# An HGRN layer by pairs of heads: the in-projection in seven products for eight

## The chip, the cores and the metric

The kernel runs on one core of one Trainium2 chip. The metric is device time in microseconds from start to end of one execution; the profile's busy times, waits and chains come from one execution taken by the hardware profiler. The engines are PE (matrix products), DVE (vector operations), ACT (functions and copies), POOL (a further vector engine) and SP, which here only issues the loads and stores.

## The reference, cut to what matters

A two-layer trunk is run over 1024 prompt frames and 32 frames of a running stream: an SSD layer, a SwiGLU FFN, an HGRN layer, a second FFN, a final norm. The change is in the HGRN layer, whose computation is:

```
proj = h @ in_w                       # (L, 1024) @ (1024, 4096)
q, f, i, g = split(proj, 4)           # 8 heads of 128 each
q = silu(q);  forget = lb + (1 - lb) * sigmoid(f);  k = 1 - forget;  logg = log(forget)
per head and chunk:  b = cumsum(logg)
    sc = mask(q*exp(b) @ (k*exp(-b))^T);  o = sc @ v + q*exp(b) @ S
    S = exp(b_last) * S + (k*exp(b_last - b))^T @ v
o = o * rsqrt(mean(o*o) + eps) * gnorm_w * silu(g)
out = o @ out_w                       # added to the residual x
```

Inputs and outputs are float32. The outputs include the carried states.

## The kernel before

**Layout.** Activations lie transposed, features on the 128 partitions and frames along the free axis. The 1056 frames are two halves: half one has 512, half two has 512 of the prompt and the 32 of the stream, 544 together (`LEN`). A block is what one matmul streams: 512 columns in half one, 272 twice in half two (`BLK`).

**Products.** Each float32 operand is split into a rounded part and a remainder (`split`, `wsplit`: a copy on ACT, a subtraction on DVE), and each product is made as three matmuls: high by high, high by low, low by high (`product`, lines 314 to 316). Weights come by DMA into `raw` (three buffers), the split weights lie in `ws` (six buffers).

**HGRN layer.** `hgrn_layer` walks 16 units, half by half, head by head. For a head, `hgrn_proj` makes one of the four parts (f, q, v, g) as a plain product of 1024 features by 128 outputs. `hgrn_f` turns f into the decay (tanh, Ln, a scan over frames at line 753, two Exp) and the keys. `hgrn_chunk` and `hgrn_chunk_b` run over four chunks of 128 frames (a fifth of 32 in half two): scores, mask, two transposes, the state's update, the output. `hgrn_gate` norms the head's output through a sum over partitions (a product with ones, line 331), Ln and Exp, and multiplies by the gate. `hgrn_out` makes the output projection of two heads and adds it to the residual (`accumulate`).

**Order.** The code is written as a list of tasks per unit that are dealt out between the chunks: g of this head, the output projection of the last two heads, f, q and v of the next head. A scheduling layer then sets the order on each engine, with some functions lifted in priority (`lifted`). Each engine runs its own list in order; semaphores tie them.

**FFN.** The FFN's gate and up products already run as units (`ffn_unit`, `unit_weights`): a matrix of 1024 by 256 weights is cut into four blocks, and seven products of sums of blocks stand for the eight (`part`, lines 993 to 995). `x_combos` makes the sums of x that these need, `unit_weights` the four sums of weights, on DVE. `in_turn` alternates the steps of two units.

Of the kernel before, what the change touches and what calls it, by code (L numbers as in the profile page):

```python
# [42 lines left out]
FIXED = 14368  # L43
BUFS = {"x": 12, "ys": 8, "cb": 4, "xd": 2, "de": 2, "ec": 2, "ss": 1, "xr": 2, "n": 4, "w": 3}
# [4 lines left out]
def trunk_kernel(ctx, tc, x_prompt, x_sample, state_ssd, cache_conv, state_hgrn,  # L49
# [85 lines left out]

    smalls, hec = [place(P) for _ in range(6)], [place(16) for _ in range(3)]
# [80 lines left out]
    cw = place(96)  # L217
    cc = place(72)
    dtb = place(1)
    acol = place(1)  # L220
    dcol = place(16)
# [30 lines left out]
    def other_vectors():  # L252
        rows = T("n", "rows")[:, :P]
        for c, src in ((C_FFN, ffn_norm_w), (C_HGN, hgrn_norm_w), (C_GN, ssd_gnorm_w),
                       (C_HG, hgrn_gnorm_w), (C_LB, hgrn_lower_bounds)):
            n = src.shape[0] * src.shape[1] // P
            dma(rows[c - NV0:c - NV0 + n, :], src.rearrange("o (m p) -> (o m) p", p=P))
        columns(rows, NVC - NV0, vc[:, NV0:])
        V.tensor_scalar_mul(vc[:, C_GN:C_HG + 1], vc[:, C_GN:C_HG + 1], 0.5)
# [76 lines left out]
    colt = place(5 * P)  # L336
# [64 lines left out]
    carry = place(NCT * 3).rearrange("p (a b) -> p a b", b=3)  # L401
    newc = place(2 * 3 * NCT).rearrange("p (a b c) -> p a b c", b=3, c=NCT)
# [21 lines left out]
    def ssd_dt(h, xn, blocks):  # L424
# [34 lines left out]
        lastc = place(5)  # L459
# [6 lines left out]
        elast = place(160).rearrange("p (h c) -> p h c", c=5)  # L466
# [181 lines left out]
    def ssd_layer(after, w0):  # L648
# [12 lines left out]
        for i, (h, g) in enumerate(units):  # L661
# [12 lines left out]
            else:  # L674
                tasks = zs + after[:1] + outs + after[1:]
# [39 lines left out]

    def half_two_norm():
# [7 lines left out]
    Sh = [Shb[e // 4][:, (e % 4) * P:(e % 4 + 1) * P] for e in range(8)]  # L724

    HB2 = 1
# [3 lines left out]
    def hgrn_proj(h, e, part, evac):  # L730
        col = (part * 8 + e) * P
        w = wload([(0, P, hgrn_in_w[0][:, col:col + P])], KD, P)
        for (b0, bn) in BLK[h]:
            ps = psum_mm()
            product(ps, w, 0, xns[h], b0, bn)
            evac(slice(b0, b0 + bn), ps[:, :bn])

    def silu2(t):
        def f(s, ps):
            act(t[:, s], ps, AF.Tanh, scale=0.5)  # L740
            stt(t[:, s], t[:, s], 1.0, ps, ADD, MUL)
        return f

    @lifted("hf")
    def hgrn_f(h, e, u):

        L = LEN[h]
        th = T("w", "hth")
        hgrn_proj(h, e, 1, lambda s, ps: act(th[:, s], ps, AF.Tanh, scale=0.5))
        d, b, k = T("w", "hlg"), T("w", "hb"), T("ys", "hk")  # L750
        act(d[:, :L], th[:, :L], AF.Ln, scale=c1[:, e:e + 1], bias=c0[:, e:e + 1])
        ts(k[:, :L], th[:, :L], nc1[:, e:e + 1], c1[:, e:e + 1], MUL, ADD)
        V.tensor_tensor_scan(out=b[:, :L], data0=rmask[:, :L], data1=d[:, :L], initial=0.0,
                             op0=MUL, op1=ADD)
        b3 = b[:, :H1].rearrange("p (c t) -> p c t", t=P)
        tt(d[:, :H1].rearrange("p (c t) -> p c t", t=P), b3,
           b3[:, :, MID:MID + 1].to_broadcast([P, 4, P]), SUB)
        if h:
            tt(d[:, H1:L], b[:, H1:L], b[:, MIDS:MIDS + 1].to_broadcast([P, NS]), SUB)
        ec = small("hec", 16)  # L760
        V.tensor_copy(ec[:, 0:4], b[:, MID:H1:P])
        V.tensor_copy(ec[:, 5:9], d[:, P - 1:H1:P])
        if h:
            V.tensor_copy(ec[:, 4:5], b[:, MIDS:MIDS + 1])
            V.tensor_copy(ec[:, 9:10], d[:, L - 1:L])
        else:
            V.memset(ec[:, 4:5], 0.0)
            V.memset(ec[:, 9:10], 0.0)
        tt(ec[:, 10:13], ec[:, 5:8], ec[:, 1:4], ADD)
        act(ec[:, :13], ec[:, :13], AF.Exp)  # L770
        ep, em = T("n", "hep"), T("n", "hem")
        act(ep[:, :L], d[:, :L], AF.Exp)
        act(em[:, :L], d[:, :L], AF.Exp, scale=-1.0)
        tt(k[:, :L], k[:, :L], em[:, :L], MUL)
        u.update(k=k, ep=ep, ec=ec)

    def hgrn_q(h, e, u):
        L = LEN[h]
        q = T("ys", "hq")
        hgrn_proj(h, e, 0, silu2(q))  # L780
        stt(q[:, :L], q[:, :L], 0.5, u["ep"][:, :L], MUL, MUL)
        u["q"] = q

    def hgrn_v(h, e, u):
        v = T("ys", "hv")
        hgrn_proj(h, e, 2, lambda s, ps: act(v[:, s], ps, AF.Copy))
        u["v"] = v

    def hgrn_g(h, e, u):
        g = T("xd", "hg")  # L790
        hgrn_proj(h, e, 3, silu2(g))
        u["g"] = g

    @lifted("hchunk")
    def hgrn_chunk(h, e, c, u):
# [17 lines left out]
        kv = T("xr", "hkv")  # L813
# [29 lines left out]
    @lifted("hgate")  # L843
    def hgrn_gate(h, e, u):
        L = LEN[h]
        ot = u["o"]
        r = rstd_of([ot[:, :L]], BLK[h], 1.0 / P, L)
        stt(ot[:, :L], ot[:, :L], vc[:, C_HG:C_HG + 1], r[:, :L], MUL, MUL)
        tt(ot[:, :L], ot[:, :L], u["g"][:, :L], MUL)
        yp = u["yp"]  # L850
        u["y"] = split(ot[:, :L], L, (yp[:, 2 * (e % 2)], yp[:, 2 * (e % 2) + 1]))

    def hgrn_out(h, e2, m4, ys):
        w = wload([(0, 512, hgrn_out_w[0][e2 * 256:(e2 + 1) * 256, m4 * 512:(m4 + 1) * 512])], 2, 512)
        for mi in range(4):
            for (b0, bn) in BLK[h]:
                ps = psum_mm()
                product(ps, w, mi * P, ys, b0, bn)
                accumulate(h, m4 * 4 + mi, ps, b0, bn)

    def hgrn_layer(after):
        units = [(h, e) for h in range(2) for e in range(8)]
        us = [{"S": None} for _ in units]
        r = []
        for f in (hgrn_f, hgrn_q, hgrn_v):
            f(0, 0, us[0])
        for i, (h, e) in enumerate(units):
            u = us[i]
            tasks = [lambda: hgrn_g(h, e, u)]
            if e % 2 == 0 and i:  # L870
                ph, pe = units[i - 1]
                tasks += [lambda m4=m4: hgrn_out(ph, pe // 2, m4, [us[i - 2]["y"], us[i - 1]["y"]])
                          for m4 in range(2)]
            if i + 1 < len(units):
                nh, ne = units[i + 1]
                tasks += [lambda f=f: f(nh, ne, us[i + 1]) for f in (hgrn_f, hgrn_q, hgrn_v)]
            if (h, e) == (0, 5):
                tasks.append(lambda: r.append(x_stat(1, st[2])))
            if (h, e) == (0, 6):
                tasks = mixed(tasks, norm_pieces(1, C_HGN, xns[1], ((0, LEN[1]),), r[0], XN2))  # L880
            if (h, e) == (1, 6):
                tasks += after[:1]
            if (h, e) == (1, 7):
                tasks += after[1:]
            u["o"] = T("ys", "ho")
# [419 lines left out]
```

## Time and profile before

| | |
|---|---|
| median of 3 runs | 2886.57 us (2885.68 to 2887.0) |
| the profiled execution | 2887.34 us, its span 2885.6 us |
| PE busy | 2843.3 us, 99% of the span |
| DVE busy | 2152.4 us, 75% |
| ACT busy | 1556.9 us, 54% |
| POOL busy | 43.5 us, 2% |
| granted clock of PE | 0.997 |

The HGRN layer lies about between 1556 and 2181 us. In a row of a group the columns are: line, engine, operation, output and inputs by the program's names, shapes, count, then busy microseconds and mean nanoseconds of one, then the engine's idle time before them and what ended it. In a row of the timeline the columns are start and duration in microseconds, then the instruction.

### The profile page before, as it was taken

The page shows a single profiled execution, that of the slowest core. Times are in us where ns is not written, and L with a number is a line of the kernel's source. Part 1 is how long each engine was busy: PE and PEld are TensorE (multiplying, and loading weights), DVE is VectorE, ACT ScalarE, POOL GpSimd, SP SyncE. Part 2 cuts the span into 40 slices and gives each one's busy share as a digit, 9 for nine tenths or more (in the row PEclk, how much of TensorE's full clock was granted, in tenths as well). Part 3 has the DMA queues.
Part 4 walks back from the last instruction along what each step waited for, and adds up shares of the span by engine and source line. Part 5 has one row for each costly group of instructions (what it writes and reads, how often), then busy time and mean ns, then how long its engine had stood idle before and what let it go on. Part 6 is the DMA issues. An engine that isn't in the chain of part 4 may idle for free.

```text
span 2885.6 us, 49044 instructions
## 1 busy us (share of the span) xinstructions
PE 2843.3 (99%) x19711; PEld 2618.5 (91%) x19711; DVE 2152.4 (75%) x3744; ACT 1556.9 (54%) x2922; POOL 43.5 (2%) x156
## 2 busy tenths in 40 slices
PE   7999999999999999999999999999999999999998
PEld 7777788999988999999999887899989999999998
DVE  6787797787787877897777556655568877887777
ACT  5665554554653744455444656555564644454445
POOL 0000000000100000000000000000000000000000
PEclk9999999999999999999999999999999999999999
DMA  5543334444332333323333222222223333333223
GB/s 152 137 111 106 98 88 123 113 112 101 107 86 88 110 104 95 110 84 102 95 96 107 81 74 66 76 78 78 73 78 95 110 96 103 107 96 96 88 89 112
DMA packets 401246, 282.60 MB, mean 98 GB/s; under 512 B 22633, under 2 KB 388730, under 8 KB 401018
## 3 DMA queue, kind: packets, MB, share of 16 engines
q1 hardware_dynamic: 401018, 279.47, 33.5%
q8 instruction: 154, 2.52, 0.4%
q14 instruction: 74, 0.61, 0.1%
HBM read 271.61 MB, written 7.82 MB: 97 GB/s over the span
## 4 chain that ended last, share of the span: by engine, by line
PE 92%; DVE 5%; ACT 1%; issue 1%; DMA 1%; SPq 0%; POOL 0%; DVEq 0%; ACTq 0%
PE mm L314 19%; PE mm L315 19%; PE mm L316 19%; PE mm L995 5%; PE mm L993 5%; PE mm L994 5%; PE sc L995 4%; PE sc L993 4%; PE sc L994 4%; PE sc L594 1%; PE sc L583 1%; PE sc L331 1%; PE sc L580 1%; DVE fixed L101 1%; PE sc L822 1%
## 5 line engine op out<-in xcount | busy, mean ns | idle before, releaser
L98 ACT ACTIVATE wh<-raw 128x512 fp32r<-128x512 f32 (+1 forms) x688 | 557.4, 818 | 604.8 <-PE mm L315 474.2
L314 PE MATMUL mm<-xn,wh 128*128 128x272 f32 (+2 forms) x1552 | 524.9, 338 | 0.0
L315 PE MATMUL mm<-xn,wh 128*128 128x272 f32 (+2 forms) x1552 | 519.3, 335 | 5.2 <-issue 5.2
L316 PE MATMUL mm<-xn,wl 128*128 128x272 f32 (+2 forms) x1552 | 518.3, 334 | 0.9 <-DVE wl L101 0.9
L101 DVE TENSOR_TENSOR wl<-raw,wh 128x1024 fp32r<-128x1024 f32 x308 | 375.8, 1222 | 82.9 <-ACT wh L98 59.3
L101 DVE TENSOR_TENSOR fixed<-mm,fixed 128x272 f32<-128x272 f32 (+1 forms) x512 | 263.2, 525 | 192.0 <-PE mm L316 190.2
L314 PE MATMUL mm<-fh,wh 128*128 128x272 f32 (+1 forms) x1056 | 341.6, 325 | 1.2 <-DVE fixed L101 0.9
L315 PE MATMUL mm<-fl,wh 128*128 128x272 f32 (+1 forms) x1056 | 341.9, 324 | 0.8 <-DVE fl L101 0.8
L316 PE MATMUL mm<-fh,wl 128*128 128x272 f32 (+1 forms) x1056 | 341.6, 324 | 0.0
L316 PEld LDWEIGHTS mm<-xn,wl 128*128 128x128 f32 x1552 | 293.4, 189 | 34.6 <-issue 6.9
L314 PEld LDWEIGHTS mm<-xn,wh 128*128 128x128 f32 x1552 | 293.3, 189 | 29.3 <-issue 2.8
L315 PEld LDWEIGHTS mm<-xn,wh 128*128 128x128 f32 x1552 | 293.2, 189 | 27.6 <-issue 1.2
L101 DVE TENSOR_TENSOR wh<-raw,wh 128x512 fp32r<-128x512 f32 x380 | 256.7, 688 | 41.5 <-ACT wh L98 38.8
L993 PE MATMUL mm<-th,wh 128*128 128x272 f32 (+1 forms) x912 | 260.4, 286 | 0.0
L995 PE MATMUL mm<-th,wh 128*128 128x272 f32 (+1 forms) x912 | 259.7, 285 | 0.0
L994 PE MATMUL mm<-tl,wh 128*128 128x272 f32 (+1 forms) x912 | 259.6, 285 | 0.0
L314 PEld LDWEIGHTS mm<-fh,wh 128*128 128x128 f32 x1056 | 198.3, 188 | 17.6 <-DVE fixed L101 1.8
L315 PEld LDWEIGHTS mm<-fl,wh 128*128 128x128 f32 x1056 | 198.7, 188 | 16.4 <-DVE fl L101 1.8
L316 PEld LDWEIGHTS mm<-fh,wl 128*128 128x128 f32 x1056 | 198.7, 188 | 15.2
L993 PE MATMUL sc<-xn,wh 128*128 128x272 f32 (+1 forms) x608 | 173.2, 285 | 0.5 <-ACT wh L98 0.5
L993 PEld LDWEIGHTS mm<-th,wh 128*128 128x128 f32 x912 | 171.8, 188 | 1.7 <-ACT s L98 0.9
L994 PE MATMUL sc<-xn,wh 128*128 128x272 f32 (+1 forms) x608 | 173.2, 285 | 0.0
(251 smaller groups left out, 6627.5 us busy)
## 6 DMA issues: line engine op xcount, KB each, us to landing
raw<-in_ffn_w_down_dram SPq DMA_DIRECT2D x90, 512.0 KB, 3.4
raw<-in_ffn_w_gate_dram SPq DMA_DIRECT2D x88, 512.0 KB, 4.1
raw<-in_ffn_w_up_dram SPq DMA_DIRECT2D x88, 512.0 KB, 4.6
raw<-in_ssd_in_w_dram SPq DMA_DIRECT2D x80, 512.0 KB, 4.1
raw<-in_hgrn_in_w_dram SPq DMA_DIRECT2D x64, 512.0 KB, 4.2
cumB<-cumd SPq DMA_DIRECT2D x64, 256.0 KB, 4.4
raw<-in_ssd_out_w_dram SPq DMA_DIRECT2D x32, 512.0 KB, 4.0
raw<-in_hgrn_out_w_dram SPq DMA_DIRECT2D x16, 512.0 KB, 3.4
```

What stands on the lines that cost most here:

```text
L98: A.activation(out=out, in_=in_, func=f, **kw)
L101: (eng or V).tensor_tensor(out=out, in0=a, in1=b, op=op)
L314: PE.matmul(ps[:, :bn], a, mh, start=(k == 0), stop=False)
L315: PE.matmul(ps[:, :bn], a, ml, start=False, stop=False)
L316: PE.matmul(ps[:, :bn], b, mh, start=False, stop=(k == n - 1))
L331: PE.matmul(ps[:, :bn], ones, tot[:, b0:b0 + bn], start=True, stop=True)
L580: PE.matmul(y23[:, j, :n], S[:, j * P:(j + 1) * P], Cx, start=True, stop=True)
L583: PE.matmul(pp, Btok[:n, :], xw[:n, :], start=True, stop=True)
L594: PE.matmul(y13[r:r + 64, i // 2, :n], xdt[:n, i * 64:(i + 1) * 64], cums[i // 4][:n, i % 4, :n], start=True, stop=True)
L993: PE.matmul(ps[:, :n], a, mh, start=(k == 0 and not more), stop=False, skip_group_check=True)
L994: PE.matmul(ps[:, :n], a, ml, start=False, stop=False, skip_group_check=True)
L995: PE.matmul(ps[:, :n], b, mh, start=False, stop=(k == 3), skip_group_check=True)
```

## The change

The layer works by pairs of heads. A part of a pair is 256 outputs wide, so it has the shape of an FFN unit, and `hgrn_unit` makes it with `unit` (the renamed `ffn_unit`) in seven products of half the frames. `merged` alternates the steps of consecutive units. The first part of each half, q of the first pair, stays a plain product (`hgrn_direct`, `hgrn_follow`), beside which the sums of x are made. With `own`, the four sums of a unit's weights are made on POOL, and one temporary is used for two. Silu replaces tanh and a product for q and g. Between two pairs, `border` puts the gates of the finished pair and the keys of the next together, function by function: squares, all Ln, then the Exp, with steps of units between. The output projection goes in halves of the frames. The gated outputs are laid into columns of the x buffers that the seven products don't read. Sums of squares of x for the next norms are spread over earlier pairs (`stat_sums`). Constants of the SSD layer move to a buffer of their own, and the convolution's cache is written at the end of the SSD layer (`conv_out`).

```diff
+    def hgrn_unit(h, p, part, tx, us):
+        u = unit(h, hgrn_src(p, part), xns[h], tx, lambda: hgrn_dst(part),
+                 lambda dst: hgrn_parts[part](h, p, us, dst), psum_h, True)
+        return [lambda: next(u, None) for _ in range(5)]
...
+    def hgrn_logs(gates, keys, us, stat):
+        if gates:
+            h, p = gates
+            for e in (2 * p, 2 * p + 1):
+                r = us[h][e]["r"]
+                for (b0, bn) in BLK[h]:
+                    ps = psum_sc()
+                    PE.matmul(ps[:, :bn], ones, r[:, b0:b0 + bn], start=True, stop=True)
+                    act(r[:, b0:b0 + bn], ps[:, :bn], AF.Ln, bias=epsc[:, 0:1], scale=1.0 / P)
...
+        if keys:
+            h, p = keys
+            for e in (2 * p, 2 * p + 1):
+                d = us[h][e]["d"]
+                act(d[:, :LEN[h]], d[:, :LEN[h]], AF.Ln, scale=c1[:, e:e + 1], bias=c0[:, e:e + 1])
...
+    def merged(units):
+        out = [(0, 0), (0, 1)]
+        for i in range(len(units)):
+            more = i + 1 < len(units)
+            out += [(i, 2)] + [(i + 1, 0)] * more + [(i, 3)] + [(i + 1, 1)] * more + [(i, 4)]
+        return [(i, s, units[i][s]) for i, s in out]
...
+        def border(gates, keys, seq, i, stat=None):
+            if gates:
+                hgrn_squares(*gates, us)
+            t = [x[2] for x in (upto(seq, i, 4) if keys else [])]
+            run(t[:1])
+            hgrn_logs(gates, keys, us, stat)
+            run(t[1:2])
+            if keys:
+                hgrn_keys(*keys, us, 0)
+            if gates:
+                hgrn_gates(*gates, us)
+            if keys:
+                hgrn_keys(*keys, us, 1)
...
+            run(t[2:])
...
-        s1 = st[NU[0] % 2][:, :512].rearrange("p (k c) -> p k c", k=4)
+        s1 = (T("xr", "s1") if own else st[NU[0] % 2])[:, :512].rearrange("p (k c) -> p k c", k=4)
+        eng = G if own else V
         yield hl(a11)
-        tt(s1, a21, a22, ADD)
+        tt(s1, a21, a22, ADD, eng)
         yield hl(s1)
         yield hl(a12)
-        tt(a21, a11, a21, SUB)
-        tt(a11, s1, a11, SUB)
+        tt(a21, a11, a21, SUB, eng)
+        tt(a11, s1, a11, SUB, eng)
         yield hl(a11)
-        tt(s1, a12, a11, SUB)
+        tt(s1, a12, a11, SUB, eng)
         yield hl(s1)
         yield hl(a21)
         yield hl(a22)
...
-    def ffn_unit(h, src, xn, tx, tag, after):
+    def unit(h, src, xn, tx, dsts, after, banks=None, own=False):
```

How the change moves instructions, at three places. In these rows stand line, operation, output and inputs with their buffer numbers, and the output's size.

POOL, from the last of the SSD layer's copies on. Before, nothing follows them:

```order
L491 COPY pre_7917<-fixed 128x3
L503 COPY fixed<-pre_7917 128x3
L504 COPY fixed<-pre_7917 128x3
L1301 UNCONDITIONAL_BRANCH
L1301 ISA
```

Now the weight sums of the units follow, four to a unit (`raw` are the loaded weights, `s` the temporary):

```order
L512 COPY ssdt<-pre_7918 128x3
L101 TENSOR_TENSOR s_2635_17341<-raw_17337,raw_17338 128x512
L101 TENSOR_TENSOR s_2648_17435<-raw_2647_17432 128x512
L101 TENSOR_TENSOR raw_17337<-raw_17337 128x4x128
L101 TENSOR_TENSOR raw_2647_17432<-raw_2647_17432 128x4x128
L101 TENSOR_TENSOR raw_17337<-s_2635_17341,raw_17337 128x4x128
L101 TENSOR_TENSOR s_2635_17341<-raw_17338,raw_17337 128x512
L101 TENSOR_TENSOR raw_2647_17432<-s_2648_17435,raw_2647_17432 128x4x128
L101 TENSOR_TENSOR s_2648_17435<-raw_2647_17432 128x512
```

Each of them works in place on weights that DVE and ACT split before and after, so POOL stands between two splits of one unit.

ACT, where a head's output is normed. Before, at the first head of half one (`sq` squares, `rstd` Ln and then Exp, `hy` the gated output, `wh` weights' rounded part):

```order
L98 ACTIVATE sq_17530<-ho_17313 128x512
L98 ACT_TABLE_LOAD
L98 ACTIVATE rstd_17532<-sc_17533,fixed 128x512
L98 ACTIVATE hkv_17548<-sc_17545 128x256
L98 ACT_TABLE_LOAD
L98 ACTIVATE rstd_17532<-rstd_17532 128x512
L98 ACTIVATE wh_17719<-raw_17717 128x1024
L98 ACTIVATE hy_17314<-ho_17313 128x512
```

Now, at the border behind the first pair (`f` is the next pair's decay, `hb` its negative exponent, `sq` both heads' statistic):

```order
L98 ACTIVATE sq_18192<-ho_17946 128x512
L98 ACTIVATE s_2737_18066<-mm_18065 128x256
L98 ACT_TABLE_LOAD
L98 ACTIVATE f_18020<-f_18020,fixed 128x512
L98 ACTIVATE sq_18190<-sc_18232,fixed 128x512
L98 ACTIVATE sq_18192<-sc_18235,fixed 128x512
L98 ACTIVATE s_2766_18241<-mm_18240 128x256
L98 ACT_TABLE_LOAD
L98 ACTIVATE sq_18190<-sq_18190 128x512
L98 ACTIVATE sq_18192<-sq_18192 128x512
L98 ACTIVATE hb_18286<-f_18020 128x512
```

Three Ln share a table load, and the Exp of both heads and of the next keys share the other.

DVE at the same two places. Before (`wl` is the weights' remainder of a plain product):

```order
L104 SCALAR_TENSOR_TENSOR ho_17313<-ho_17313,fixed,rstd_17532 128x512
L101 TENSOR_TENSOR ho_17313<-ho_17313,hg_17323 128x512
L832 TENSOR_SCALAR fixed<-sc_17584,fixed 128x128
L809 COPY_PREDICATED fixed<-fixed,sc_17590 128x128
L101 TENSOR_TENSOR wl_17720<-raw_17717,wh_17719 128x1024
L101 TENSOR_TENSOR hy_17314<-ho_17313,hy_17314 128x512
```

Now (`xn` is the gated output in the x buffer, the row of L970 frees a PSUM bank of the next pair's first chunk):

```order
L101 TENSOR_TENSOR fixed<-fixed,g_17688 128x512
L101 TENSOR_TENSOR ho_17946<-ho_17946,g_17689 128x512
L101 TENSOR_TENSOR hk_18180<-hk_18180,hb_18286 128x512
L101 TENSOR_TENSOR xn<-fixed,xn 128x2x256
L101 TENSOR_TENSOR xn<-ho_17946,xn 128x2x256
L101 TENSOR_TENSOR q_17854<-q_17854,f_18020 128x512
L101 TENSOR_TENSOR v_18195<-s_2737_18066 128x256
L101 TENSOR_TENSOR g_18373<-mm_18317,s_2766_18241 128x256
L101 TENSOR_TENSOR wh_18378<-raw_18242,wh_18378 128x512
L101 TENSOR_TENSOR wh_18395<-s_2769_18246,wh_18395 128x512
L946 COPY_PREDICATED fixed<-fixed,sc_18461 128x128
L970 TENSOR_SCALAR fixed<-sc_18411,fixed 128x128
```

Both heads' gates, the second head's keys and the splits of three units' weights now stand in one run ahead of that row, where before one head's gate lay between chunk operations.

More of the change, by code (lines that the diff above doesn't have):

```diff
@@ L752, in hgrn_f @@
[L752 to L759, printed above, removed]
@@ L841, in hgrn_chunk_b @@
             dma(hgrn_p[0, 0, e], dst)
[L843 to L859, printed above, removed]
@@ L1049, in in_turn, with two @@
             prev = u
+    def two(tag):
+        return [T(tag, "f" + tag) for _ in range(2)]
     def ffn_gate(layer, h, s, xn, tx, g):
```

429 lines of the change are left out of this document (291 added, 138 removed).

## The prediction

> **What bounds the kernel now.** I read the engine totals, the chain of waits, the busy time by stretch, then the groups of the HGRN layer, 1556 to 2181 us. First the page: totals, and the chain by engine.
>
> ```profile
> PE 2843.3 (99%) x19711; PEld 2618.5 (91%) x19711; DVE 2152.4 (75%) x3744; ACT 1556.9 (54%) x2922; POOL 43.5 (2%) x156
> PE 92%; DVE 5%; ACT 1%; issue 1%; DMA 1%; SPq 0%; POOL 0%; DVEq 0%; ACTq 0%
> ```
>
> PE is the bound: a matmul taken out is time won, as long as the others keep up. By stretch (PE, PEld, DVE, ACT, POOL busy, then clock, DMA): the layer, and a stretch of the second FFN, which already multiplies by seven products for eight.
>
> ```profile
> 1556.00:2181.00 625.00, 620.50 (x3904) 555.08 (x3903) 375.56 (x748) 357.70 (x586) 0.00 (x0) 1.00 0.28 79
> 2480.00:2850.00 370.00, 368.40 (x2874) 364.96 (x2873) 285.35 (x497) 177.32 (x328) 0.00 (x0) 1.00 0.30 91
> ```
>
> The layer has DVE 60% and ACT 57% busy, PE idle for 4.5 us. The FFN runs DVE at 77% with PE idle for 1.6 of 370 us: seven products need not starve PE.
>
> **What the change takes from PE.** Matmuls overlap, so their price is the distance of starts: the first and last row of unbroken runs (6 steps, 23 steps, 12 steps), and one group of the layer.
>
> ```profile
> 1662.41 0.39 PE L314 MATMUL mm<-hy,wh 128*128 128x512 f32 x1
> ...
> 1663.79 0.39 PE L314 MATMUL mm<-hy,wh 128*128 128x512 f32 x1
> 2700.07 0.29 PE L993 MATMUL mm<-th,wh 128*128 128x272 f32 x1
> ...
> 2702.96 0.29 PE L995 MATMUL mm<-th,wh 128*128 128x272 f32 x1
> 1031.76 0.28 PE L993 MATMUL mm<-th,wh 128*128 128x256 f32 x1
> ...
> 1033.18 0.28 PE L993 MATMUL sc<-xn,wh 128*128 128x256 f32 x1
> L314 PE MATMUL mm<-h,wh 128*128 128x272 f32 x512 | 150.6, 294 | 0.0
> ```
>
> So 230 ns for 512 columns, 126 for 272, 118 for 256. Half one's in-projection is 4 parts x 8 heads x 24 = 768 matmuls of 512; half two's is 1536 of 272 (the group's 512, three lines). Afterwards 30 of 32 pair products are units of 7 x 12 = 84 matmuls of half width: 1260 of 256 and 1260 of 272. One pair product of each half stays plain: 48 of 512, 96 of 272. The output projection of half one, now in halves, goes from 192 of 512 to 384 of 256. Together -912 of 512 (-209.8 us), -180 of 272 (-22.6), +1644 of 256 (+194.5): **-38 us**. Chunk products and sums over partitions are as many as before.
>
> **What it adds on DVE and ACT.**
>
> ```profile
> L101 DVE TENSOR_TENSOR wl<-raw,wh 128x1024 fp32r<-128x1024 f32 x93 | 113.5, 1222 | 15.5 <-ACT wh L98 11.9 <-issue 3.2
> L101 DVE TENSOR_TENSOR wh<-raw,wh 128x512 fp32r<-128x512 f32 x380 | 256.7, 688 | 41.5 <-ACT wh L98 38.8
> L104 DVE SCALAR_TENSOR_TENSOR hg<-hg,mm 128x272 f32<-128x272 f32 x16 | 7.0, 435 | 17.8 <-ACT hg L98 17.8
> L104 DVE SCALAR_TENSOR_TENSOR hg<-hg,mm 128x512 f32<-128x512 f32 x8 | 5.4, 680 | 0.0
> L101 DVE TENSOR_TENSOR xt<-xf,xt 128x256 f32<-128x256 f32 x4 | 1.7, 422 | 0.0
> L101 DVE TENSOR_TENSOR fixed<-mm,fixed 128x272 f32<-128x272 f32 x64 | 26.9, 439 | 13.2 <-PE mm L316 12.8
> L98 ACT ACTIVATE wh<-raw 128x1024 fp32r<-128x1024 f32 x308 | 324.2, 1056 | 408.9 <-PE mm L315 333.7 <-issue 28.6 <-DMA raw<-in_ssd_in_w_dram 16.1
> L98 ACT ACTIVATE wh<-raw 128x512 fp32r<-128x512 f32 x380 | 234.5, 625 | 195.9 <-PE mm L315 140.5 <-DMA raw<-in_ffn_w_up_dram 29.0 <-PE sc L995 7.9
> L98 ACT ACT_TABLE_LOAD x70 | 89.8, 1283 | 15.1 <-DVE fixed L761 14.0
> L98 ACT ACTIVATE s<-mm 128x256 f32<-128x256 f32 x108 | 40.2, 377 | 20.3 <-PE mm L995 19.6
> ```
>
> DVE: 60 splits of 1024 columns go (-73 us), 210 of 512 come (+144); silu's 32 + 16 products of tanh with PSUM go (-25); 45 sums per half of the units at 0.42 or 0.44 (+39); sums of x for 16 more tiles, with splits (8 x 0.69, 32 halves at 0.43, 16 splits at about 0.7: +31); the output projection accumulates 64 halves for 32 wholes (+5). Sum **+121 us**, 376 to 497. ACT: copies -63 and +131, evacuations with silu and tanh in place of tanh from PSUM about +47, 16 sums split +10, table loads 70 to 40, as they stand in ACT's order (-38): about +87, 358 to 445. Beside 620.5 - 38 = 582 us of PE that is DVE 85%, ACT 76%: more than the FFN stretch's 77% of DVE, and the layer has chains that the FFN lacks. What else moves keeps its count and lies beside PE's stream: the squares of x for the next norms go into earlier pairs, and the two transposes and two copies of the convolution's cache go into the last SSD unit; I cost both at nothing (uncovered, the cache's part would be under 1 us). Weight bytes are unchanged: 64 loads of 512 KB, from two queues of buffers as in the FFN, so I cost SP's order at nothing; a load that came late would cost its landing, 4.2 us at the median:
>
> ```profile
> raw<-in_hgrn_in_w_dram SPq DMA_DIRECT2D x64, 512.0 KB, 4.2
> ```
>
> **POOL is new here.** The four sums of a unit's weights, on DVE in the FFN, go to POOL: 120 tensor_tensor of 128x512, behind which the splits of three of seven products wait. The trace has no such row. Nearest: POOL's tensor_tensor of 128x4 at 1.0 us, and copies of 128x3 that take 0.19 us, or 1.70 when DVE works through operations with two SBUF inputs.
>
> ```profile
> L101 POOL TENSOR_TENSOR fixed<-fixed 128x4 f32<-128x4 f32 x1 | 1.0, 1007 | 1.1 <-DVE fixed L107 1.1
> 220.37 0.19 POOL L500 COPY fixed<-pre 128x3 f32<-128x3 f32 x1 [7.82 <-ACT pre L98]
> 227.36 1.70 POOL L500 COPY fixed<-pre 128x3 f32<-128x3 f32 x1 [6.76 <-ACT pre L98]
> 226.06 2.36 DVE L101 TENSOR_TENSOR wl<-raw,wh 128x1024 fp32r<-128x1024 f32 x2
> 228.33 0.69 DVE L104 SCALAR_TENSOR_TENSOR ca<-cth,ca 128x512 f32<-128x512 f32 x1
> ```
>
> The copy of 227.36 ends at 229.06, when DVE's operation of 228.33 has ended at 229.02, and DVE's durations are its usual ones: here POOL waits for DVE and DVE loses nothing. [...] I take 1 us per sum and 0.2 us of it lost on DVE (between 0 and 1.0), so DVE 521 of 582: nearly full, not the bound.
>
> **Where PE will wait.** At each of 7 borders between pairs, the gates of one pair and the keys of the next stand together. From the partition sums (L862) to the first gated product on PE stand 64 matmuls of 256 columns and half a microsecond of a chunk: 64 x 0.118 + 0.6 = 8.2 us. Beside it runs the chain, priced by these:
>
> ```profile
> L98 ACT ACTIVATE rstd<-sc,fixed 128x512 f32<-128x512 f32 x9 | 6.2, 688 | 0.9 <-PE sc L331 0.8
> L98 ACT ACTIVATE rstd<-rstd 128x512 f32<-128x512 f32 x9 | 5.7, 632 | 0.1
> L104 DVE SCALAR_TENSOR_TENSOR ho<-ho,fixed,rstd 128x512 f32<-128x512 f32 x8 | 6.0, 752 | 18.1 <-ACT rstd L98 18.1
> L101 DVE TENSOR_TENSOR ho<-ho,hg 128x512 f32<-128x512 f32 x8 | 5.5, 690 | 0.2
> ```
>
> Two Ln 1.4, a copy 0.4, a table load 1.3, two Exp 1.3; two products 1.5, two by the gate 1.4, a key product 0.7, two splits 1.4: 9.4 us, one more than the cover. Behind them on DVE stand a q product, two evacuations, two weight splits and a mask (0.7 + 0.8 + 1.4 + 0.3 = 3.2 us) before the row that frees the PSUM bank of PE's next chunk, four matmuls on: PE waits about 1 + 3 = 4 us there. In half two the free bank comes later in PE's order, and I make it 1 to 2 us. I take **3 us per border, 21 in all** (0 to 6 each: the scheduler hides all, or POOL's waits come on top). At the start DVE has 17.8 us for the sums of x (8 x 0.69, 16 x 0.42, 8 x 0.69) plus 8 of other work, against 8 x 12 x 0.126 + 48 x 0.230 = 23 us of PE: 2.5 us late; half two's norm with its sums, 3 us. Sum of waits 26.5, in place of the 4.5 us idle now: +22.
>
> **Sum:** -38 + 22 = -16 us on the profiled execution's 2887.3 (span 2885.6, 1.7 around it), which is 0.8 above the median of runs: **2870 us**.
>
> **Rivals.** (1) All waits hidden, as in the FFN stretch: -38 - 4.5 = -42, 2844. For it: the keys' first head is hoisted into the chunks before the border. Against: DVE at 85% where the FFN has 77%. (2) The borders eat the gain: 5 us each, 35 + 5.5 - 4.5 = 36 lost, -2, 2885. For it: the 4 us that I count at the first border have no semaphore delay in them. (3) Slower: DVE becomes the bound because POOL's sums hold it up. It decides from (582 - 497) / 120 = 0.7 us lost per sum; at the 1.0 us of POOL's row DVE has 617 us, and with what it waits for Ln before its scans,
>
> ```profile
> DVE hb L753 <- ACT hlg L98: 19.2, 16, 1.6
> ```
>
> 636 us, +11: 2898. For it: three products of each unit depend on those sums. Against: in the rows above POOL waits and DVE doesn't. [...] (4) The half-wide products don't run at their pace: excluded by the FFN's rows.
>
> **Chances.** My forecast 0.50 (own range 2857 to 2881), rival 1 0.17, rival 2 0.13, rival 3 0.20. What this measurement can tell from no change is about 0.2%, 5.8 us: faster 0.67, same 0.13, slower 0.20. The range reaches from rival 1 to just past rival 3's first price: 2843 to 2902.
>
> **What would show it.** Matmuls of the layer at 118 and 126 ns from start to start; DVE near 500 us in the layer; 40 table loads; PE idle before the output projection's first product and before the chunk after each border, released by DVE. I am wrong if PE's idle time stands inside the units, released by splits that wait for POOL (rival 3), if DVE's durations grow, or if the layer ends less than 38 us earlier with PE never idle.

## The result, and the profile after

The changed kernel takes 2914.8 us at the median of 4 runs (2911.0 to 2915.3), the kernel before 2886.8 beside it: the ratio is 1.0093, with a 95% interval from 1.0075 to 1.0110. It is 28 us slower; the forecast was 17 faster, and the time lies above the range. First the totals and the chain by engine, of the page after:

```profile
PE 2829.7 (97%) x20263; PEld 2637.5 (91%) x20263; DVE 2322.5 (80%) x4024; ACT 1629.4 (56%) x3169; POOL 227.0 (8%) x276
PE 83%; DVE 9%; ACT 4%; issue 2%; DMA 1%; POOL 0%; SPq 0%; DVEq 0%; ACTq 0%; POOLq 0%
```

PE is busy for 14 us less than before, but it was 92% of the chain that ended last and is now 83%, DVE and ACT taking what it lost. The layer now stands between 1560 and 2215 us. By stretch (length; PE, PEld, DVE, ACT, POOL busy; clock; DMA):

```profile
1560.00:2215.00 655.00, 609.18 (x4434) 575.91 (x4433) 544.37 (x1023) 427.24 (x831) 182.64 (x120) 0.97 0.24 75
```

It is 30 us longer than before. PE is idle for 46 of 655 us (4.5 of 625 before), at a mean clock of 0.97 (1.00 before), while no other engine is full: DVE is at 83%. POOL works for 183 us, and DVE's operations have become longer. In the groups by shape of the layer (busy, mean ns of one, idle before):

```profile
L101 POOL TENSOR_TENSOR raw<-s,raw 128x512 f32<-128x512 f32 x30 | 47.6, 1587 | 127.3 <-DVE wh L101 95.8 <-DVE fixed L891 12.4 <-DVE fixed L892 8.9
L101 POOL TENSOR_TENSOR s<-raw 128x512 f32<-128x512 f32 x30 | 44.9, 1497 | 143.1 <-DMA raw<-in_hgrn_in_w_dram 90.9 <-DVE wh L101 28.9 <-PE mm L1209 7.9
L101 DVE TENSOR_TENSOR wh<-raw,wh 128x512 fp32r<-128x512 f32 x150 | 133.6, 895 | 18.6 <-ACT wh L98 17.8
L107 DVE TENSOR_SCALAR hk<-f,fixed 128x512 f32<-128x512 f32 x8 | 10.2, 1278 | 0.1
L101 DVE TENSOR_TENSOR fixed<-mm,fixed 128x272 f32<-128x272 f32 x58 | 24.5, 434 | 3.4 <-PE mm L324 2.8
```

A split took 688 ns before and takes 895 here; an addition with a PSUM operand takes 434 for 439, as before. One stretch of the timeline shows how PE comes to wait (start, duration, instruction, idle before it and what ended that):

```profile
1585.90 3.72 POOL L101 TENSOR_TENSOR raw<-s,raw 128x512 f32<-128x512 f32 x1 [8.91 <-ACT th L98]
...
1587.78 0.69 DVE L101 TENSOR_TENSOR wh<-raw,wh 128x512 fp32r<-128x512 f32 x1
1589.65 0.63 ACT L98 ACTIVATE wh<-raw 128x512 fp32r<-128x512 f32 x1 [2.93 <-POOL raw L101]
1589.70 1.27 POOL L101 TENSOR_TENSOR s<-raw,raw 128x512 f32<-128x512 f32 x1
1590.32 1.20 DVE L101 TENSOR_TENSOR wh<-raw,wh 128x512 fp32r<-128x512 f32 x1 [1.85 <-ACT wh L98]
1591.01 0.63 ACT L98 ACTIVATE wh<-s 128x512 fp32r<-128x512 f32 x1 [0.72 <-POOL s L101]
...
1593.06 0.37 ACT L98 ACTIVATE s<-mm 128x256 f32<-128x256 f32 x1
...
1593.48 0.39 PE L1207 MATMUL mm<-th,wh 128*128 128x256 f32 x1 [3.30 <-ACT s L98]
```

POOL's sum of 1585.90 stands beside a train of DVE operations and ends only at 1589.62, 1.15 us after the last of them (the shortest of the 120 sums takes 1.27). ACT's copy of that sum waits for it for 2.93 us, and behind that copy in ACT's list, after four other operations, stands the evacuation `s<-mm` on which PE's next product depends. Then the roles turn: the split of 1590.32 runs beside the sum of 1589.70 and takes 1.20 us in place of 0.69. PE stands for 3.30 us.

Two sums over the trace are used below. **PE over its pace**: of each matmul the distance to the next start, less the median of that distance for its line and shape, summed over the layer; it holds idle time, slow clock and uneven starts. **DVE's lengthening**: the duration less that of the fastest tenth of its form, where that is over 0.1 us.

| layer of | length | PE over its pace | DVE lengthened |
|---|---|---|---|
| before | 624.8 us | 19.0 us | 0 |
| after | 655.1 us | 89.9 us | 86 us, 103 operations |

Without what is over the pace PE's work fell from 605.8 to 565.2 us, by 41. The loss is the 71 us that came in on top: 41 us of it are idle time (46 for 4.5) and some 20 are slow clock (last section); the rest is not taken apart.

### The profile page after: what moved, and what is told of

Its sections match the earlier page's. It is cut to its first block, busy times and chain, and to the rows that moved or that the text cites. A ratio compares the mean times of both kernels' runs of the same rounds, so it can differ in the third digit from the quotient of the medians.

```text
span 2913.2 us, 51104 instructions
## 1 busy us (share of the span) xinstructions
PE 2829.7 (97%) x20263; PEld 2637.5 (91%) x20263; DVE 2322.5 (80%) x4024; ACT 1629.4 (56%) x3169; POOL 227.0 (8%) x276
## 4 chain that ended last, share of the span: by engine, by line
PE 83%; DVE 9%; ACT 4%; issue 2%; DMA 1%; POOL 0%; SPq 0%; DVEq 0%; ACTq 0%; POOLq 0%
PE mm L322 14%; PE mm L324 14%; PE mm L323 14%; PE mm L1207 7%; PE mm L1209 7%; PE mm L1208 7%; PE sc L1209 4%; PE sc L1208 4%; PE sc L1207 4%; DVE wh L101 1%; DVE fixed L101 1%; PE sc L602 1%; PE sc L591 1%; DMA raw<-in_ssd_in_w_dram 1%; PE sc L588 1%
## 5 line engine op out<-in xcount | busy, mean ns | idle before, releaser
L98 ACT ACTIVATE wh<-raw 128x512 fp32r<-128x512 f32 (+1 forms) x778 | 586.7, 762 | 514.0 <-PE mm L323 368.3
L322 PE MATMUL mm<-xn,wh 128*128 128x272 f32 (+2 forms) x1520 | 490.9, 323 | 1.6 <-DVE g L101 1.6
L323 PE MATMUL mm<-xn,wh 128*128 128x272 f32 (+2 forms) x1520 | 483.4, 318 | 4.4 <-issue 4.4
L324 PE MATMUL mm<-xn,wl 128*128 128x272 f32 (+2 forms) x1520 | 482.6, 318 | 1.0 <-DVE wl L101 0.9
L101 DVE TENSOR_TENSOR wh<-raw,wh 128x512 fp32r<-128x512 f32 x530 | 390.1, 746 | 66.5 <-ACT wh L98 63.1
L1207 PE MATMUL mm<-th,wh 128*128 128x272 f32 (+1 forms) x1392 | 404.5, 291 | 15.4 <-ACT s L98 9.0
L101 DVE TENSOR_TENSOR fixed<-mm,fixed 128x272 f32<-128x272 f32 (+2 forms) x544 | 267.6, 502 | 175.6 <-PE mm L324 173.3
L1209 PE MATMUL mm<-th,wh 128*128 128x272 f32 (+1 forms) x1392 | 400.2, 287 | 0.0
L1208 PE MATMUL mm<-tl,wh 128*128 128x272 f32 (+1 forms) x1392 | 399.2, 287 | 0.0
L101 DVE TENSOR_TENSOR wl<-raw,wh 128x1024 fp32r<-128x1024 f32 x248 | 303.1, 1224 | 76.3 <-ACT wh L98 52.5
L1207 PEld LDWEIGHTS mm<-th,wh 128*128 128x128 f32 x1392 | 264.8, 190 | 20.2 <-ACT s L98 11.9
L1208 PEld LDWEIGHTS mm<-tl,wh 128*128 128x128 f32 x1392 | 264.7, 190 | 0.6 <-issue 0.2
L1209 PEld LDWEIGHTS mm<-th,wh 128*128 128x128 f32 x1392 | 265.0, 190 | 0.2
```

The source lines that it names most:

```text
L98: A.activation(out=out, in_=in_, func=f, **kw)
L101: (eng or V).tensor_tensor(out=out, in0=a, in1=b, op=op)
L322: PE.matmul(ps[:, :bn], a, mh, start=(k == 0), stop=False)
L323: PE.matmul(ps[:, :bn], a, ml, start=False, stop=False)
L324: PE.matmul(ps[:, :bn], b, mh, start=False, stop=(k == n - 1))
L1207: PE.matmul(ps[:, :n], a, mh, start=(k == 0 and not more), stop=False, skip_group_check=True)
```

## The experiments

Theory A: POOL's sums hold DVE up through something that the two share, 86 us in 120 sums. Theory B: the chains at the seven borders between pairs hold PE. Theory C: DVE is over-full from its own work. Each run stands beside runs of the kernel before on its chip (medians 2883.7 to 2884.7), so differences to that are compared: +28.0 us for the changed kernel.

### Where the sums are made

```diff
-        eng = G if own else V
+        eng = V
```

> The four weight sums of each of the 30 units go to DVE, as in the FFN; nothing else is changed. After the change DVE's operations in the layer stand 86 us above their usual lengths while POOL works 183 us. Theory A (POOL's sums hold DVE up through what the two share, and come late to the splits): DVE gets 120 x 0.69 = 83 us of work of its own and loses the 86 us, a sum is there 0.7 us after its inputs in place of 1.5, so DVE is no fuller than now and its durations are back at 0.69 us per split: 2885 to 2900. Theory B (the chains at the seven borders hold PE): they do not change, 2910 to 2920. Theory C (DVE is over-full from its own 497 us, POOL is harmless): with 580 us of its own it is the bound, 2930 or more.

Measured 2876.6 us, 7.7 less than before: ratio 0.9975 (0.9966 to 0.9984). The one word wins 36 us over the changed kernel, and this kernel is faster than both. The lengthening is 0; PE is 52 us over its pace.

```profile
1563.00:2180.00 617.00, 596.74 (x4429) 564.76 (x4429) 530.71 (x1140) 426.59 (x830) 0.00 (x0) 0.99 0.25 79
```

DVE does 120 more operations than after the change, and is busy for 14 us less. B and C fall; of A the direction is borne out, while its price was too high (2885 to 2900). The profiled execution was the longest of ten (2882.4), so its rows are rather long.

```diff
+        if own:
+            for x in (a11, a21, a12, a11, a21, a21, a22):
+                yield hl(x)
+            return
```

> The four weight sums of a unit are left out: its seven products split the loaded quarters of the weights instead (so the in-projection's values are not the reference's; loads, splits, products and additions are as many as before). POOL has nothing to do in the layer. Theory A: DVE's lengthening of 86 us goes, and with it most of PE's 46 us of idle time: 2865 to 2880, the forecast of the prediction. Theory B: the borders remain, 2900 to 2915. Theory C: DVE's own 497 us remain, 2900 or more.

Measured 2866.3 us, 17.9 less than before (ratio 0.9936, 0.9921 to 0.9951): without the sums the change wins about what was forecast for it, 17. DVE, with all its other new work, is busy for 462 of 603 us, and PE is 38.8 us over its pace, 20 more than before the change.

```profile
1562.00:2165.00 603.00, 586.54 (x4432) 556.51 (x4431) 461.89 (x1022) 424.69 (x831) 0.00 (x0) 1.00 0.26 81
```

### Hold or lateness

```diff
+            yield hl(a11)
+            tt(s1, a21, a22, ADD, eng)
+            yield hl(a21)
+            yield hl(a12)
+            tt(s1, a11, a21, SUB, eng)
+            tt(s1, a22, a11, SUB, eng)
+            yield hl(a11)
+            tt(s1, a12, a11, SUB, eng)
+            yield hl(a21)
...
```

> POOL does its four sums per unit as now, from the same loaded weights, but into a buffer that nobody reads: the seven products split the loaded quarters (values are not the reference's). So POOL still runs beside DVE, and no split waits for a sum. If what costs is that POOL's operations lengthen DVE's (the lock): DVE's durations stay lengthened by some 0.7 us per sum and the time is within 10 us of the changed kernel's 2915. If what costs is the wait of the splits for late sums: the time is that of the kernel without sums, 2865 to 2880. Theory B: 2900 to 2915 here as there.

Measured 2938.5 us, 54.3 more than before. In this kernel and the last PE, ACT and DVE do the same instructions, in nearly the same order (21 of DVE's 4024, 11 of ACT's 3169 and 47 of PE's 20263 stand elsewhere); the one difference in work is 120 sums on POOL that nobody reads, and they cost 72 us, 0.60 each. Splits behind the first border in the two timelines, first without and then with the sums:

```profile
1615.63 2.49 DVE L101 TENSOR_TENSOR wh<-raw,wh 128x512 fp32r<-128x512 f32 x4
```

```profile
1620.90 6.93 POOL L101 TENSOR_TENSOR s<-raw 128x512 f32<-128x512 f32 x4 [15.15 <-DMA raw<-in_hgrn_in_w_dram]
1621.45 0.42 DVE L101 TENSOR_TENSOR g<-mm,s 128x256 f32<-128x256 f32 x1
1621.79 7.20 DVE L101 TENSOR_TENSOR wh<-raw,wh 128x512 fp32r<-128x512 f32 x5
```

Four splits took 2.49 us, 0.62 each. Beside POOL four sums take 6.93 and five splits 7.20 us, and taken singly four of each alternate: the sums end at 1622.71, 1624.44, 1626.16 and 1627.83, the splits at 1623.27, 1624.99, 1626.71 and 1628.38, each about 0.55 us after a sum. So one sum and one split end in 1.72 us, where a sum with no DVE operation beside it takes 1.29 (six of the changed kernel's) and splits alone start about 0.6 apart: in these rows the two take turns, with little overlap, and this is what the expectation's "lock" comes to in the runs. The fifth split, behind the last of the sums, takes 0.68. The operation with a PSUM operand keeps its 0.42 us. So the hold on DVE alone is enough for the loss, and no split needs to wait for a sum. That the time is even longer than the changed kernel's I put down to the row of four: the sums start together when a load lands, while in the changed kernel they wait for splits (95.8 us in the first POOL row above). That is argued from the rows, not tested.

```diff
+            cp1 = lambda x: G.tensor_copy(s1, x)
...
-            tt(s1, a21, a22, ADD, eng)
+            cp1(a21)
...
```

> As the run with the unread sums (the products split the loaded quarters, so values are not the reference's), but POOL's four operations per unit are copies of 128x512, with one operand read in place of two. The same buffers are held, so it also tells a hold on the loaded weights from a hold on DVE. If any POOL operation on these buffers holds DVE up, or if holding the loaded weights longer is what costs: 2925 to 2940 as there. If it takes an operation with two operands read: 2866 to 2872, as without sums, and DVE's durations at 0.69 us.

Measured 2873.1 us, 11.7 less than before and 6 more than without the sums. The lists of PE and ACT are here those of the run with the unread sums, and DVE's differ in one place (a split and two fills of one column): between these two lie 66 us, and only the operation on POOL differs. The copies read the same buffers, if for a shorter time, and in the layer of the unread sums no wait of PE or ACT was ended by a load, so late loads are not the cause. The splits, of the layer's groups, with the sums unread and with the copies (687 ns without either):

```profile
L101 DVE TENSOR_TENSOR wh<-raw,wh 128x512 fp32r<-128x512 f32 x210 | 173.2, 838 | 34.9 <-ACT wh L98 34.0
```

```profile
L101 DVE TENSOR_TENSOR wh<-raw,wh 128x512 fp32r<-128x512 f32 x210 | 148.5, 720 | 41.4 <-ACT wh L98 40.3
L1191 POOL COPY s<-raw 128x512 f32<-128x512 f32 x120 | 101.5, 855 | 1209.2 <-DMA raw<-in_hgrn_in_w_dram 1076.6 <-ACT f L98 30.2 <-PE mm L1223 22.8
```

A copy lengthens DVE too, by 22 us in all or 0.18 each, against 99 us or 0.82 for a sum. Expected was none or all; it is about a fifth.

### Dose, and a DVE with room

```diff
-        eng = G if own else V
+        eng, eng2 = (G if own else V), V
...
-        tt(a11, s1, a11, SUB, eng)
+        tt(a11, s1, a11, SUB, eng2)
         yield hl(a11)
-        tt(s1, a12, a11, SUB, eng)
+        tt(s1, a12, a11, SUB, eng2)
```

> The first two of a unit's four weight sums stay on POOL, the other two go to DVE: 60 sums on POOL in place of 120, values unchanged. With all on POOL the time was 2915, with none 2877. Theory A with a price per sum (each POOL sum costs DVE about 0.7 us, and a sum on DVE costs DVE as much): the loss halves, 2890 to 2900, and DVE's lengthening falls from 86 to about 43 us. If only the late sums count, those that a split waits for (the last two): close to 2877. If the mere presence of POOL in a unit counts: close to 2915.

Measured 2898.8 us, 14.1 more than before. From none (-7.7) over 60 (+14.1) to 120 (+28.0): 22 us for the first 60 sums, 14 for the others; the lengthening is 46 us of 86. That fits a price per sum, and not the last two sums alone: taking these from POOL won less than half. It does not by itself exclude lateness, since all four are waited for: of a unit's seven splits the second and the sixth read the sums that stayed, the fourth and the fifth those that went.

```diff
-        w = wload([(0, P, hgrn_in_w[0][:, col:col + P])], KD, P)
+        raw = wraw([(0, P, hgrn_in_w[0][:, col:col + P])], KD)
+        w = wsplit(raw, KD)
+        for _ in range(2):
+            G.tensor_tensor(out=st[3][:, :512], in0=raw[:, :512], in1=raw[:, 512:], op=ADD)
```

> The kernel before, and in its HGRN layer POOL adds the two halves of each of the 64 loaded weight tiles twice, 128 tensor_tensor of 128x512, into a buffer that nobody reads; nothing else is changed and the values are the reference's. DVE is busy there for 374 of 625 us. If a POOL sum costs its 0.8 us of DVE wherever DVE stands, and PE waits only when DVE is full: DVE goes to some 470 of 625, below the 83% at which the changed kernel lost time, and the time stays within 10 us of 2885. If each sum that hits a split or a mask delays PE directly, full or not (72 us for 120 sums in the pair of runs with the same order of instructions): 2935 to 2960.

Measured 2903.8 us, 20.1 more than before (ratio 1.0070, 1.0055 to 1.0085): 0.16 us per sum, between the two expectations. PE, ACT and DVE do the same instructions in the same order as before. The stretch of the layer, and the group of the sums:

```profile
1562.00:2206.00 644.00, 626.95 (x3875) 556.47 (x3874) 422.55 (x742) 356.72 (x585) 193.89 (x128) 0.99 0.26 76
```

```profile
L735 POOL TENSOR_TENSOR fixed<-raw 128x512 f32<-128x512 f32 x128 | 193.9, 1515 | 1151.8 <-DVE xf L104 798.2 <-DMA raw<-in_hgrn_in_w_dram 347.1
```

DVE has a third of its time free and still PE loses 20 us, with DVE lengthened by 53 us, 0.41 per sum. DVE need not be full for POOL to cost time. A sum cost more where DVE was fuller (0.16 here, 0.60 for the unread sums in the changed kernel, whose DVE is at 77% without them), but the two kernels differ in more than that, so this is no rule yet.

### The borders

> The kernel without weight sums, and besides it the norm of the gates is left out (squares, their sums over partitions, Ln, Exp; the gate is still multiplied by its gain and by silu), so that of the borders' chain only the products by the gate, the splits and the keys are left; values are not the reference's. PE loses 24 sums over partitions, 8 x 0.230 + 16 x 0.126 = 3.9 us. Prediction's border term (3 us per border, from the gates' chain): 2866 - 4 - 14 to 21 = 2841 to 2848. If PE's remaining 39 us over its steady pace come from elsewhere (evacuations and splits inside the units, as in the run's trace about 0.9 us per 30 us also between borders): 2858 to 2864.

Left out are `hgrn_squares`, the products with ones and their Ln, and the Exp of `hgrn_gates`. Measured 2844.5 us, 22.3 less than without the sums alone; it looks like the border term, but the expectation had priced PE's part at 3.9 us, and that was wrong. A product of `ones` with float32 squares is two passes, as the rows without the sums show (the first of a border, and four passes in a row):

```profile
1654.22 1.02 PE L862 MATMUL sc<-sq,fixed 128*128 128x512 f32 x2
1858.56 1.88 PE L862 MATMUL sc<-sq,fixed 128*128 128x512 f32 x4
```

Some 0.5 us per pass of 512 columns, where a pass of the split products takes 0.23. By the steady distances PE's work fell by 13.6 us, and what is over its pace only by 5.0 (38.8 to 33.8). So of the 20 us that the pair structure adds without the sums, the norm's chain at the borders makes 5. The keys' chain stays at the borders in this run, and no run leaves it out. But in the kernel without the sums PE is over its pace by 12 of its 39 us around the pairs of scans (9 us before the first to 6 after the second, together 235 of 603 us), so the borders are no worse than the rest of the layer. Of its 16.5 us of idle time 7 stand before products of units, 4 before chunk products and 5 before plain products.

> The 30 units become plain products (as the one plain pair product of each half), in the same places of the pair structure, and the sums of x for the units are left out: gates of a pair and keys of the next still stand together at seven borders, POOL has no sums, and the values are the reference's. PE has the in-projection of before, about 1 us more for the output projection in halves. Theory A (the borders cost what the prediction says or less, POOL the rest): 2887 + 1 + 0 to 21 = 2888 to 2908. Theory B (the borders' chains cost the 60 to 70 us that are lost): 2940 or more.

The edit puts `hgrn_direct` in the place of `hgrn_unit` in `stages`. Measured 2919.2 us, 34.9 more than before, between the two expectations. Against what the expectation says, its values are not the reference's; I put that down to the plain products taking their result buffers two steps earlier than units do, which is not tested. DVE is at 54% and the layer's clock at 0.98; PE's waits are of another kind, few and long (the longest of them in the timeline, and the group):

```profile
2042.49 0.82 PE L322 MATMUL mm<-xn,wh 128*128 128x272 f32 x2 [8.11 <-ACT xn L98]
```

```profile
L322 PE MATMUL mm<-xn,wh 128*128 128x272 f32 x592 | 178.8, 304 | 25.4 <-ACT xn L98 15.1 <-ACT wh L98 10.3
```

Four of them, of 5 to 8 us, stand between 1868 and 2124 us, from the border into half two on, and end with ACT's gated products (`xn` in half two) or splits. The gates' chain does stop PE when the steps of two units do not cover it. Because the buffers go round otherwise too, I take nothing more from this run.

### Can the better version be bettered

Three more edits of the kernel with the sums on DVE. First, work from DVE to ACT:

```diff
-            ts(k[:, :L], t[:, :L], nc1[:, e:e + 1], c1[:, e:e + 1], MUL, ADD)
+            act(k[:, :L], t[:, :L], AF.Identity, scale=nc1[:, e:e + 1], bias=c1[:, e:e + 1])
...
-            V.tensor_scalar_mul(dst, t, f)
+            act(dst, t, AF.Copy, scale=f)
```

> The four sums on DVE, and two kinds of operation go from DVE to ACT: the linear map that makes a key (16) and the scaling of a head's state (64); values are the reference's. DVE loses 16 x 0.55 + 64 x 0.28 = 27 us, ACT gets 16 x 0.63 + 64 x 0.27 = 27. With the sums on DVE the time was 2877 and DVE was busy for 531 of 617 us; without the sums 2866 and 462 of 603: 10 us for 69. If DVE's fill is what separates these two: -4, about 2872. If it is the sums' place in the chain from a load to its split: 2876 to 2878. If ACT (427 of 617) becomes the one that is waited for: 2880 or more.

> The four sums on DVE, and only the 16 linear maps that make the keys go to ACT; the scaling of a head's state stays on DVE. The run with both moved took 2896, and its PE waited for ACT's scaled state ahead of the chunk products (11.6 and 4.6 us in its gaps). If the state's way over ACT was what cost there: 2873 to 2878, the 9 us of DVE saved against 13 us of ACT. If ACT's load is what costs, whatever is added: 2885 or more.

Both edits: 2896.1 us, 11.4 more than before. The keys alone: 2892.5, 8.7 more than before and 16 more than with the keys on DVE. So the expectation for the second run fails: the state's way over ACT adds only 3 us, and the keys' 13 us on ACT (821 ns each, 545 on DVE) cost more than their own length. The rows of the chunk products, with the sums on DVE, with both edits, and with the keys alone, show one place where it goes:

```profile
L960 PE MATMUL sc<-fixed 128*128 128x128 f32 x128 | 25.7, 282 | 3.3 <-ACT fixed L98 2.8 <-ACT v L98 0.5
```

```profile
L960 PE MATMUL sc<-fixed 128*128 128x128 f32 x128 | 26.7, 291 | 15.1 <-ACT fixed L98 15.1
```

```profile
L960 PE MATMUL sc<-fixed 128*128 128x128 f32 x128 | 26.3, 288 | 9.0 <-ACT fixed L98 8.8
```

PE waits there for a copy of ACT, though ACT is busy for only 439 of 631 us with the keys alone. That points to the place in ACT's list and not to its load, but it is 6 us of the 16, and no run shows it apart. Each edit also moves other instructions in the lists, so the sizes are not those of the moved work alone.

```diff
-        act(u["o"][:, o:o + n], po[:, :n], AF.Copy)
+        V.tensor_copy(u["o"][:, o:o + n], po[:, :n])
```

> The opposite of the runs that moved work from DVE to ACT: with the four sums on DVE (2877), the 64 copies of a chunk's output out of PSUM go from ACT (0.27 us each, 17 us) to DVE (about 0.28 each, 18 us); values are the reference's. Moving 13 us of the keys from DVE to ACT had cost 16 us of time. If what PE waits for is ACT's place in the order (copies that free PSUM banks and first halves of splits): 2865 to 2873. If DVE's fill is the limit after all (531 of 617 us busy, 549 then): 2880 to 2890. If both have slack and the order that follows from each edit decides: 2873 to 2880, and the two earlier moves to ACT stay unexplained in size.

The other way costs too: 2883.9 us, no change against before (0.9999, 0.9989 to 1.0008), 7 us lost for 17 moved. By the expectation's second case DVE's fill counts, here 0.4 us per us; adding 83 us of sums had cost 10, and in that trace five stretches at half clock, 17 us together, make some 8 us. The runs don't give one price for DVE.

```diff
-    HP = dict(norm=600, gate=100, hgate=0, chunk=0, hchunk=50, hchunkb=0, dt=0, wl=0, hf=0, conv=0)
+    HP = dict(norm=600, gate=100, hgate=0, chunk=0, hchunk=150, hchunkb=0, dt=0, wl=0, hf=0, conv=0)
```

> The four sums on DVE, and the first part of a chunk's instructions is set 150 places ahead in the order in place of 50 (the priority named hchunk); the work is the same. PE's gaps of the run with the sums on DVE stand ahead of units' products, released by splits and evacuations, about as often as ahead of chunk products (6 us of 44). If the chunk's mask and copy are what is late: 2868 to 2874. If the units' splits are: 2876 to 2885, since the chunk's work then goes ahead of them on DVE.

Measured 2875.7 us, 8.0 less than before (0.9971, 0.9961 to 0.9982): the same as with the sums on DVE alone, at the edge of both expectations. PE is 48.7 us over its pace for 51.8.

## Why the prediction was wrong, step by step

**The step that failed** is "I take 1 us per sum and 0.2 us of it lost on DVE (between 0 and 1.0), so DVE 521 of 582: nearly full, not the bound". It has two faults. The size: a sum took 1.52 us at the mean, and DVE was lengthened by 0.72 us per sum (86 us by 120). And what follows from it: as long as DVE is not full, the forecast let POOL cost PE nothing, 24 us of DVE's time and none of PE's, and at 0.72 it would still have come out at about nothing. Between the changed kernel and the one without sums lie 46 us of time, with DVE busy for 83%. Take the 46 away and the changed kernel stands 18 us below the kernel before, where the forecast had 17. That the rest meets the forecast so well is in part luck, as the terms below show.

The 0.2 came from one copy of three columns that waited for DVE ("here POOL waits for DVE and DVE loses nothing"). A row in which one side loses says nothing of the other side: in the alternating rows each waits in its turn, and a copy of 0.19 us could have cost DVE little more than that. No run shows the 0.2: a sum cost DVE 0.41 us in the kernel before, 0.72 in the changed kernel and 0.82 where nobody read it. Nor does any show a sum at 1 us, the length of POOL's operation on four columns: even the six sums of the changed kernel beside which no DVE operation ran took 1.29. Not every DVE operation grew: one with a PSUM operand kept its length (434 for 439 ns). And it was not only those that read two tensors: the keys' map, with one tensor and two scalars per partition, went from 545 ns (sums on DVE) to 1278. What POOL does counts too: a copy there took 0.86 us at the mean and cost DVE 0.18, a sum that nobody read 1.55 and 0.82.

**Rival 3** had the mechanism and the wrong condition. It was to decide "from 0.7 us lost per sum", where DVE's time fills PE's. The loss was 0.72, at which by that sum nothing would yet be lost, and DVE was busy for 83% only. DVE's total does not decide: the kernel before with POOL's sums lost 20 us with DVE at 66%. What does, by the waits in the timelines, is when a single split or evacuation ends: one that comes late stops PE although DVE has idle time later, and behind a copy that waits for POOL stands whatever is next in ACT's list. The prediction also counts three products of a unit behind the sums; four of its seven splits read one. Rival 3's price, 2898, lies 17 us below the result.

**PE's price** held: 41 us less work by the steady distances (without the sums the same), forecast 38.

**DVE's own work** was right as a sum of durations, 118 us for the forecast 121, and too high as busy time. "376 to 497" adds durations to a busy time; successive DVE records overlap by some 0.09 us (four of 0.69 us start 0.60 apart at 1585.97 and after), and the busy time counts that once. Without sums DVE was busy for 462 us. It made rival 3 look nearer to its condition than it was, and hid that DVE was not what had to be full. ACT's 445 were 427, the 40 table loads 43.

**The waits at borders, start and norm** met their size by luck: +22 us forecast, and without the sums PE is 20 us more over its pace than before, 12 of them idle time (16.5 for 4.5). Only 5 of the 20 come from the norm's chain at the borders; the rest is spread over the layer, and the forecast had that at nothing. The terms for the start and for half two's norm were not measured singly. In the changed kernel 20 of the 46 us of idle time stand before products of units, most of them ended by ACT's evacuations and splits, and 18 before chunk products. The waits inside the units, with DVE's longer operations, are the sign that the prediction had named for rival 3. Rival 2 in its own form, long stops at the borders, showed only where plain products stood in the units' place. Rival 1 (2844) is out of reach by some 20 us, even without the sums.

**What was in no part of the prediction** is the clock, below: it added some 20 us beside the 46 of idle time.

## What to carry to other kernels

Before work goes from VectorE to GpSimd, look at what VectorE does meanwhile. Here, with float32 operations that read SBUF on both, the two took turns in the rows shown, and a sum on the "free" engine cost VectorE 0.72 us where its own sum takes 0.69, and arrived late besides; one word, the sums back on VectorE, turned 0.9% slower into 0.25% faster. An engine at 66 or 83% can still be what TensorE waits for: count what stands ahead of the next product in each list, not only busy time. When a trace shows one side of a contention, price the other side by the same rule until a run says otherwise.

## What the runs showed of the hardware beyond that

**Ten times in the layer PE ran at half clock after short stops.** Its granted clock fell to 0.97 in the layer after the change, 0.96 with the unread sums, and stayed at 1.00 without sums. After the stop of 3.30 us that ends at 1593.48, after one of only 1.67 us that ends at 1611.62, and after one of 1.71 us that ends at 1866.00, by stretches of 2 us (the clock is the column after the busy times):

```profile
1594.00:1596.00 2.00, 2.00 (x14) 2.00 (x14) 2.00 (x3) 1.26 (x3) 0.74 (x1) 0.69 0.00 0
1596.00:1598.00 2.00, 2.00 (x12) 2.00 (x11) 2.00 (x3) 0.90 (x2) 1.28 (x1) 0.50 0.65 183
1598.00:1600.00 2.00, 2.00 (x18) 2.00 (x18) 1.93 (x4) 1.70 (x4) 0.84 (x1) 0.96 0.35 109
...
1613.00:1615.00 2.00, 2.00 (x11) 2.00 (x11) 1.23 (x1) 1.32 (x4) 0.00 (x0) 0.50 0.36 68
...
1866.00:1868.00 2.00, 2.00 (x16) 2.00 (x17) 2.00 (x5) 1.54 (x3) 0.64 (x1) 1.00 0.46 132
1868.00:1870.00 2.00, 2.00 (x19) 2.00 (x18) 1.12 (x2) 0.00 (x0) 2.00 (x1) 1.00 0.39 142
```

The timeline about the stop of 1.67 us, its first matmul and the last of those at half clock:

```profile
1611.62 0.42 PE L1207 MATMUL mm<-th,wh 128*128 128x256 f32 x1 [1.67 <-ACT s L98]
1611.84 0.41 PE L1208 MATMUL mm<-tl,wh 128*128 128x256 f32 x1
...
1615.04 0.38 PE L1209 MATMUL mm<-th,wh 128*128 128x256 f32 x1
1615.25 0.28 PE L1207 MATMUL mm<-th,wh 128*128 128x256 f32 x1
1615.37 0.28 PE L1208 MATMUL mm<-tl,wh 128*128 128x256 f32 x1
```

For 3.4 us (1611.62 to 1615.04) matmuls start 0.21 us apart in place of 0.12, which costs 1.5 us, about as much again as the stop. After the stop of 1.71 us the clock stays at 1.00, so the length alone does not decide. The trace's record of the granted clock has ten stretches at half clock in the layer, of 3.41 or 6.83 us, and they begin at 1594.76, 1611.83, 1628.89 and so on, always whole multiples of 3.41 us apart. In the steps of that grid at full clock PE was idle for 1.67 us or more in each one ahead of a fall, and for 1.59 us or less in every other, about half a step; the two groups lie only 0.08 us apart in this one trace, so it gives no sharp limit. The ten stretches are 44 us together, by estimate (half of it) some 20 us of the 71 lost.

**The float32 products with ones cost about four times a split pass.** One of 512 columns is two passes of some 0.5 us, where a split pass of as many takes 0.23; leaving 24 such products out took 13.6 us of work from PE. They were there before the change as well, so they bear on neither verdict.
